# Inverse products spread over four row strips, and score products of a half gathered in one burst, in a two-layer hybrid trunk (pooling, retention, RWKV-7)

## The chip, the cores and the metric

The kernel runs on one core of a Trainium2 chip. The metric is the device time of one execution in microseconds. It is measured several times, and the median is taken. The profile is one further execution on the chip, taken by the hardware profiler.

The engines are named as in the profile: PE is TensorE (matmuls), PEld its weight loads, DVE VectorE, ACT ScalarE, POOL GpSimd, SP the queue that issues the DMAs. PSUM is the memory into which PE writes.

## What is computed

Two layers run one after the other on 1024 positions of 1024 channels, and a last RMSNorm follows. In a layer the normalised input goes through one wide projection, whose columns feed three token mixers: a causal pooling mixer, a retention mixer, and an RWKV-7 time mixer with 8 heads of 64 channels. Each mixer's output is gated, projected back, weighted by a sigmoid gate for each channel, summed, projected once more and added to the input. All is float32.

The change lies in the RWKV-7 mixer. Its definition goes step by step over the positions, with a 64 x 64 state S for each head:

```python
def step(S, inp):
    r_t, w_t, k_t, v_t, a_t, b_t = inp
    sa = jnp.einsum('bhvk,bhk->bhv', S, a_t)
    S = (S * w_t[:, :, None, :] + sa[..., None] * b_t[:, :, None, :]
         + v_t[..., None] * k_t[:, :, None, :])
    return S, jnp.einsum('bhvk,bhk->bhv', S, r_t)
_, y = lax.scan(step, jnp.zeros((B, H, N, N), jnp.float32), xs)
```

The kernel does it in chunks of 64 positions. In a chunk the recurrence is a triangular system, so each chunk and head needs the inverse of a 64 x 64 matrix that is the identity plus a strictly triangular part.

## The kernel before, in words

**The big projections.** The weights are streamed from DRAM in tiles (`wr`). Each tile is split into a high and a low part (`wh`, `wl`) of the fast fp32r type, and the activations are kept split in the same way (`hhi`, `hlo`). One fp32 product of 512 columns is then three fp32r matmuls into a PSUM tile `acc` (`mm3`). These acc products are most of PE's work and run all along.

**The RWKV task.** `rwkv_task` (line 1206 on) is called for a pair of heads, four times a layer, eight times in all. The heads of a pair lie in rows 0 to 63 and 64 to 127 of the tiles. A task has these stages, with 16 chunks of 64 positions:

- For each half of the sequence (8 chunks) it prepares the scaled operands `AR` and `BK`. LoRA products go into `lw` and `la`; transposes follow (`vt`, `bt`).
- *Score products g* (lines 1302 to 1318): BK times AR for each chunk and head, 64 rows deep and 128 x 128 in size. The two heads use the two 64-row halves of the array. Before, they come in two groups q of four chunks, eight products in each, into two PSUM tiles (one `mx`, one `cy`), and DVE masks them into `Z`, `GQ` and `KG` after each group.
- *The inverse* (lines 1338 to 1367): each 64 x 64 triangle is cut into four blocks of 32 x 32. DVE inverts the diagonal blocks by 30 elimination steps on `VB` and transposes the results into `GQ` and `N_` (a view of `Z`).
- *The products m1 and m2* (lines 1370 to 1390): the off-diagonal block of the inverse is (inverse of one diagonal block) x (off-diagonal block) x (inverse of the other), so two 32 x 32 products for each of 16 chunks x 2 heads. m1 reads rows 0 to 31, m2 reads rows 32 to 63. Each comes as two groups of 16, and ACT copies each group out of PSUM.
- *The chain over the chunks* (from line 1405): for c = 0 to 15 it alternates products `cy` and `ch` on PE with small copies on DVE and ACT. The first `ch` reads the finished inverse in `GQ`.

**What sets the order.** All operations are first recorded. The recording follows a clock of its own: the acc products call `pump()`, which lets tasks of the lanes ("rwkv", "mix", "norm", "post", "ada") record their next piece whenever its due time has come; `wait` delays a piece until the planner believes its inputs to be ready. `Prog.needs` then derives which operation depends on which. `Prog.weave` (line 406) is a list scheduler: it prices each operation (`Prog.cost`, line 347), and puts the operation of the engine that is free first next in the program. So each engine's order is fixed before the kernel runs, and on the chip each engine goes through it in that order. The helper at line 549 emits all instructions, so every row of the profile has this line, and the tiles' names tell the rows apart. The profile leaves out digits in names: m1 and m2 both read `m`, and `t_mq("mn")`, `t_mq("mt")` of the change read `mn` and `mt`.

The kernel divides PSUM into eight tiles of 512 columns: three `acc`, two `mx`, two `cy`, one `ch`.

Of the kernel before, what the change touches and what calls it, by code (L numbers as in the profile page):

```python
# [18 lines left out]
P = 128  # L19
# [187 lines left out]

class Op:
    __slots__ = ("eng", "what", "args", "kw", "outs", "ins", "prio", "lane", "pred", "succ", "n", "i",
                 "dur", "occ", "load", "twice", "lock", "est", "start", "end", "left", "table", "acc", "arr", "seq", "know", "waits", "part")  # L210


class Engine:
# [47 lines left out]
class Prog:  # L261


    def __init__(self):
        self.ops, self.bufs, self.width, self.pools = [], [], {}, {}
        self.now = lambda: 0.0
        self.lane = [None]
        for e in ENG:
            setattr(self, e, Engine(self, e))

# [40 lines left out]
    def needs(self):  # L311
        uses = {}
        for o in self.ops:
            for views, write in ((o.ins, False), (o.outs, True)):
                for v in views:
                    if v.tensor.key is not None:
                        uses.setdefault(v.tensor, []).append((o, v.mask(), write))
        for chain in self.chains.values():
            old = []
            for b in chain:  # L320
                w, r, mine = [], [], []
                for o, m, write in uses[b]:
                    free = True
                    for q, x in w:
                        if x & m and q is not o:
                            o.pred[q.i] = "d"
                            free = False
                    if not write:
                        r.append((o, m))
                    else:  # L330
                        for q, x in r:
                            if x & m and q is not o:
                                o.pred.setdefault(q.i, "a")
                                free = False
                        r = [(q, x & ~m) for q, x in r if x & ~m]
                        w = [(q, x & ~m) for q, x in w if x & ~m] + [(o, m)]
                    if free:
                        for q, wrote in old:
                            if q is not o:
                                o.pred.setdefault(q.i, "w" if wrote and write else "a")  # L340
                    mine.append((o, write))
                old = mine
        for o in self.ops:
            for q in o.pred:
                self.ops[q].succ.append(o.i)

    def cost(self, o):
# [6 lines left out]
        if o.eng == "PE":  # L354
            n = o.outs[0].free_size()
            rhs = o.ins[1]
            k = rhs.index.shape[0] * 32
            o.twice = rhs.dtype != F32R and w != "transpose"
            if rhs.dtype == F32R:
                o.load, o.occ, o.dur = (107, (n + 32) / 2.4, n / 2.4 + 176) if k == 128 else (55, 116, 393)  # L360
            elif k == 128:
                o.load, o.occ, o.dur = 109, 53, 273 if n > 1 else 250
            else:
                o.load, o.occ, o.dur = (55, 53, 272) if k == 64 else (32, 32, 191)
            return
        if o.eng == "SP":
            o.occ, o.dur = 470, 2100 if o.ins[0].space != DRAM and o.ins[0].tensor.key else 2650
# [38 lines left out]
    def weave(self):  # L406
# [9 lines left out]
        for o in ops:  # L416
            if not o.left:
                o.waits = []
                ready[o.eng].append(o)
        landed, table, pe = [0.0] * 8, 0, [0.0, 0.0]  # L420
        work = [0.0] * (int(WARM_UP / WINDOW) + 2)
        order = []
        other = {"DVE": "POOL", "POOL": "DVE"}
# [8 lines left out]
        while len(order) < len(ops):  # L432
# [23 lines left out]
            if e == "PE":  # L456
                k = int((s + 1000) / WINDOW) if s < WARM_UP else -1
                slow = 2 if k == 0 or k > 0 and work[k - 1] < 0.78 * WINDOW else 1
                ld, c = o.load * slow, c * slow
                m = max(pe[1], max(pe[0], o.est) + ld)  # L460
                if o.twice:
                    m += max(ld, c)
                if k >= 0:
                    work[k] += (m + c - max(s, pe[1])) * (1 if o.outs[0].free_size() > 1 else 0.1)
                pe[:] = m, m + c
                o.start, o.end = m, m + d + c - o.occ
            else:
                o.start, o.end = s, s + d
                free[e] = s + (d if e in over else c)
# [11 lines left out]
            for i in o.succ:  # L481
                p = ops[i]
                kind = p.pred[o.i]
                if p.eng != e or e == "SP":
                    r = o.end + SPACE_LAT[p.eng]
                elif kind != "a" and e != "PE":
                    r = o.end + SPACE_LAT[e]
                else:
                    r = s
                if r == s:  # L490
                    p.est = max(p.est, r)
                else:
                    a = p.arr.get(src, (0.0, 0, False))
                    p.arr[src] = max(a[0], r), max(a[1], o.seq), a[2] or kind == "d"
                    if kind == "d" and e != "SP":
                        for k, n in o.know.items():
                            if k != p.eng and n > p.know.get(k, 0):
                                p.know[k] = n
# [54 lines left out]
def trunk_kernel(ctx, tc, xT, cvec, pos, vecs, consts, w_ada, w_all, pool_w, lora_w, out):  # L553
# [19 lines left out]
    def nm(s):  # L573
        uid[0] += 1
        return f"{s}_{uid[0]}"
# [11 lines left out]
    t_mo = slot("mo", 4, HF + 16)  # L587
    t_vp = slot("vp", 2)
    t_cs = slot("cs", 3)
    mi = lambda s: t_mi(s)[:, 0:HF]  # L590
    mo = lambda s: t_mo(s)[:, 0:HF]

# [6 lines left out]

    def cyt(s):  # L600
        return ps_c.tile([P, HF], F32, tag="cy", name=nm(s))

    def hb(s):
        return hp_.tile([P, HF], F32R, tag="hb", name=nm(s))
# [601 lines left out]
    def rwkv_task(l, hp, kT, rT, vp, lt, lw):  # L1206
# [18 lines left out]
        for h in range(2):  # L1225
# [69 lines left out]
            for q in range(2):  # L1295
                ps = mx("bt")
                c0 = 8 * h + 4 * q
                for c in range(4):
                    trans(ps[:, c * P : (c + 1) * P], jt(BK, slice(0, P), c0 + c))
                nc.scalar.copy(BKt[:, c0 : c0 + 4, :], ps.rearrange("p (c n) -> p c n", n=P))  # L1300
                yield 1300
            for q in range(2):
                c0 = 8 * h + 4 * q
                yield wait(AR)
                gps = [mx("g"), cyt("g")]
                for j in range(4):
                    for hd in range(2):
                        rows = slice(64 * hd, 64 * hd + 64)
                        mmul(gps[hd][:, j * P : (j + 1) * P], jt(BK, rows, c0 + j), jt(AR, rows, c0 + j))
                lo, hi = slice(0, 64), slice(64, 128)  # L1310
                for hd in range(2):
                    own, other = (lo, hi) if hd == 0 else (hi, lo)
                    g3 = gps[hd].rearrange("p (u n) -> p u n", n=P)
                    c4 = slice(c0, c0 + 4)
                    nc.vector.tensor_tensor(Z[lo, c4, own], g3[lo, :, lo], rm(lo, lo), op=ALU.mult)
                    nc.vector.tensor_tensor(GQ[own, c4, hi], g3[lo, :, hi], rm(lo, hi), op=ALU.mult)
                    nc.vector.tensor_tensor(KG[other, c4, :], g3[hi, :, :], rm(hi, slice(0, P)), op=ALU.mult)
# [15 lines left out]
        def place_values(hd):  # L1333
            rows, cols = slice(64 - 64 * hd, 128 - 64 * hd), slice(64 * hd, 64 * hd + 64)
            nc.gpsimd.memset(VB[rows, :, 64 - 64 * hd : 128 - 64 * hd], 0.0)
            nc.scalar.copy(VB[rows, :, cols], Z[64:128, :, cols])

        place_values(0)
        for b in range(2):
            q = slice(32 * b, 32 * b + 32)  # L1340
# [20 lines left out]
            out=GQ[0:32, :, 0:64].rearrange("p a (b s) -> p s a b", s=32),  # L1361
            in_=M[0:32, :].rearrange("p (a b s) -> p s a b", s=32, b=2),
        )
        for b in range(2):
            q = slice(32 * b, 32 * b + 32)
            nc.vector.transpose(
                out=N_[q, :, q].rearrange("p u t -> p t u"), in_=M[q, :].rearrange("p (t s) -> p t s", s=32)
            )
        place_values(1)
        yield 2000  # L1370
        yield wait(Zt, G)
        for q in range(2):
            ps = mx("m1")
            for u in range(16):
                uu = 16 * q + u
                mmul(ps[32:64, u * 32 : u * 32 + 32], N_[0:32, uu, 32:64], t1(slice(0, 32), uu))
                if u % 16 == 15:
                    yield 600
            nc.scalar.copy(GQ[32:64, 8 * q : 8 * q + 8, 0:64], ps[32:64, :].rearrange("p (c n) -> p c n", n=64))
        yield wait(G)  # L1380
        for q in range(2):
            ps = mx("m2")
            for u in range(16):
                uu = 16 * q + u
                mmul(ps[0:32, u * 32 : u * 32 + 32], t1(slice(32, 64), uu), N_[32:64, uu, 32:64])
                if u % 16 == 15:
                    yield 600
            nc.scalar.copy(
                N_[0:32, 16 * q : 16 * q + 16, 32:64], ps[0:32, :].rearrange("p (u s) -> p u s", s=32)
            )  # L1390
        nc.vector.tensor_copy(GQ[0:64, :, 0:64], Z[0:64, :, 0:64])
        nc.scalar.copy(GQ[64:128, :, 0:64], Z[0:64, :, 64:128])
        SS = [sp.tile([P, P], F32, tag="S", name=nm("S"), bufs=2) for _ in range(2)]
        for S in SS:
            nc.gpsimd.memset(S, 0.0)
# [9 lines left out]
        for c in range(16):  # L1405
# [13 lines left out]
            if c < 15:  # L1419
                cy_next = own_values(c + 1)  # L1420
            yield wait(xst)
            ch = ps_c.tile([P, HF], F32, tag="ch", name=nm("ch"), bufs=1)
            mmul(ch[:, 0:P], GQ[:, c, :], xst)
            nc.vector.tensor_copy(Z[0:64, c, :], ch[0:64, 0:P])
            for hd in range(2):
# [712 lines left out]
```

## Time and profile before

| | |
|---|---|
| median of 3 runs | 2336.88 us (2336.01 to 2342.26) |
| the profiled execution's own time | 2333.52 us |
| its span, first to last instruction | 2331.7 us |
| granted TensorE clock, mean | 0.996 of full speed |
| DRAM traffic over the span | 97 GB/s |

In the profile the busy time of an engine is a share of the span. A weight load (PEld) overlaps the matmuls (PE). A matmul row's length is that of one instruction through the pipeline, and the next one starts long before it ends, so the cost of a matmul is read from start to start. An fp32 matmul appears as two records, one for each pass, and an fp32r matmul as one. A row of the timeline with a count holds that many records one after the other.

### The profile page before, as it was taken

What the parts mean: (1) busy time and instruction counts of PE and PEld (TensorE: products, weight loads), DVE (VectorE), ACT (ScalarE), POOL (GpSimd) and SP (SyncE); (2) the same over time, 40 slices, a digit from 0 to 9 for tenths busy, and PEclk for the clock granted to TensorE, in tenths of its full rate; (3) what the DMA queues carried; (4) which work ended last, traced back from release to release, by engine and by line L of the source; (5) the groups of instructions that cost most, each with busy time, mean ns of one, the idle gap of its engine ahead of it and who ended that gap; (6) DMA issues with size and microseconds to landing.
All of it is one profiled execution on the core that took longest, in us unless ns stands there. A gap on an engine that the chain in (4) does not pass through costs nothing. (4 is left out here: it accounts for less than half of the span.)

```text
span 2331.7 us, 33818 instructions
## 1 busy us (share of the span) xinstructions
PE 2287.5 (98%) x12520; PEld 1907.6 (82%) x12520; DVE 1442.1 (62%) x2826; ACT 855.8 (37%) x1706; POOL 817.4 (35%) x714
## 2 busy tenths in 40 slices
PE   5999999999999999999999999999999999999998
PEld 4888888888888888888887888888788888888888
DVE  8776578468568744669546746855864884413544
ACT  5633442433433333223444334234433423311343
POOL 5222233234142333463442233323323333326441
PEclk9999999999999999999999999999999999999999
DMA  8132112112213325767422211211211131545442
GB/s 283 39 110 78 42 46 92 42 41 70 73 55 99 102 61 178 237 194 250 139 82 64 69 41 44 94 34 49 78 61 42 56 118 52 162 126 163 118 145 82
DMA packets 126517, 227.79 MB, mean 98 GB/s; under 512 B 14352, under 2 KB 17680, under 8 KB 126352
## 3 DMA queue, kind: packets, MB, share of 16 engines
q1 hardware_dynamic: 126352, 225.63, 30.9%
q8 instruction: 98, 1.61, 0.3%
q14 instruction: 67, 0.55, 0.1%
HBM read 176.56 MB, written 49.02 MB: 97 GB/s over the span
## 5 line engine op out<-in xcount | busy, mean ns | idle before, releaser
L549 PE MATMUL acc<-hhi,wh 128*128 128x512 f32 x2000 | 806.7, 403 | 0.0
L549 PE MATMUL acc<-hhi,wl 128*128 128x512 f32 x2000 | 806.6, 403 | 0.0
L549 POOL TENSOR_TENSOR wl<-wr,wh 128x512 fp32r<-128x512 f32 x342 | 458.5, 1341 | 991.4 <-ACT wh L549 947.3
L549 PE MATMUL acc<-hlo,wh 128*128 128x512 f32 x2000 | 805.1, 403 | 0.0
L549 ACT CAST wh<-wr 128x512 fp32r<-128x512 f32 x342 | 212.2, 620 | 655.2 <-PE acc L549 441.7
L549 PEld LDWEIGHTS acc<-hlo,wh 128*128 128x128 f32 x2000 | 378.0, 189 | 66.6 <-issue 2.2
L549 PEld LDWEIGHTS acc<-hhi,wl 128*128 128x128 f32 x2000 | 378.1, 189 | 66.5 <-issue 2.2
L549 PEld LDWEIGHTS acc<-hhi,wh 128*128 128x128 f32 x2000 | 378.2, 189 | 65.6 <-issue 1.1
L549 PE MATMUL acc<-oG,wl 128*128 128x512 f32 x384 | 149.9, 390 | 0.0
L549 PE MATMUL acc<-oG,wh 128*128 128x512 f32 x384 | 149.7, 390 | 0.0
L549 PE MATMUL acc<-olo,wh 128*128 128x512 f32 x384 | 149.7, 390 | 0.0
L549 DVE SCALAR_TENSOR_TENSOR S<-ch,pc,SP 64x64 f32<-64x64 f32 x224 | 63.3, 282 | 91.3 <-PE ch L549 85.2
L549 ACT COPY xst<-Z 64x64 f32<-64x64 f32 x256 | 62.4, 244 | 152.7 <-DVE Z L549 149.5
L549 DVE COPY xst<-cy 64x64 f32<-64x64 f32 x256 | 55.4, 216 | 90.7 <-PE cy L549 65.2
L549 DVE TENSOR_TENSOR tm<-VB 64x30 f32<-64x30 f32 (+14 forms) x240 | 105.4, 439 | 7.4
L549 DVE TENSOR_TENSOR VB<-VB,tm 64x30 f32<-64x30 f32 (+14 forms) x240 | 99.4, 414 | 7.5
L549 DVE COPY Z<-ch 64x128 f32<-64x128 f32 x128 | 36.0, 282 | 93.1 <-PE ch L549 92.5
L549 ACT ACTIVATE gsg<-acc 128x512 f32<-128x512 f32 x88 | 52.4, 596 | 91.9 <-PE acc L549 79.6
L549 PEld LDWEIGHTS acc<-olo,wh 128*128 128x128 f32 x384 | 72.1, 188 | 15.0
L549 PEld LDWEIGHTS acc<-oG,wh 128*128 128x128 f32 x384 | 72.1, 188 | 15.0 <-DVE gs L549 0.2
L549 PEld LDWEIGHTS acc<-oG,wl 128*128 128x128 f32 x384 | 72.1, 188 | 15.0
L549 DVE SCALAR_TENSOR_TENSOR gs<-gs,acc 128x512 f32<-128x512 f32 x64 | 43.7, 684 | 46.1 <-PE acc L549 45.0
(270 smaller groups left out, 3693.6 us busy)
## 6 DMA issues: line engine op xcount, KB each, us to landing
wr<-in_w_all SPq DMA_DIRECT2D x364, 256.0 KB, 2.7
gd<-gsg SPq DMA_DIRECT2D x88, 256.0 KB, 2.0
gs<-gd SPq DMA_DIRECT2D x88, 256.0 KB, 2.8
wada<-in_w_ada SPq DMA_DIRECT2D x70, 256.0 KB, 3.3
ol<-od SPq DMA_DIRECT2D x64, 256.0 KB, 3.2
ringG<-in_w_ada SPq DMA_DIRECT2D x26, 256.0 KB, 5.1
x<-in_xT SPq DMA_DIRECT2D x16, 256.0 KB, 5.0
od<-po SPq DMA_DIRECT2D x16, 256.0 KB, 2.2
```

The source lines that it names most:

```text
L549: f(*[put(x) for x in o.args], **{k: put(x) for k, x in o.kw.items()})
```

## The change

The score products of one half of the sequence are issued together: sixteen products into four PSUM tiles (`mx`, `cy`, `ch`, `cy`) where before there were two groups of eight, each with two tiles. DVE masks them after that, in the same operations as before.

The products m1 and m2 are spread over the four strips of 32 rows. Strip g holds one head of the pair and one half of the chunks (the list `quad`): eight products in each strip. The operands of three of the four strips are therefore copied into two new tiles `mn` and `mt` (W1 and W2 in the code) by ACT and DVE, partly before the inversion, partly after it. The products of a step are issued as one list of 32, in which each product is on another strip than the one before. Each strip has its own PSUM tile. Each result is copied out in four pieces of 32 x 256, two by ACT and two by DVE, where before there were two pieces by ACT. The result of m2 now goes straight into `GQ`, and the copies of the diagonal blocks into `GQ` are recorded between the two steps.

For the scheduler, the products of such a list are recorded as a burst: each product of a burst is given the dependences of all of them, so that the list starts when all its operands are there. The price of a pass with 32 rows goes from 32 to 15 ns, and a change of the number of rows between two products costs 110 ns (to 32 rows) or 200 ns.

```diff
+        for a, b in self.bursts:
+            own = [o for o in self.ops[a:b] if o.eng == "PE"]
+            union = {q for o in own for q in o.pred if not a <= q < b}
+            for o in own:
+                for q in union:
+                    o.pred.setdefault(q, "x")
...
-                o.load, o.occ, o.dur = (55, 53, 272) if k == 64 else (32, 32, 191)
+                o.load, o.occ, o.dur = (55, 53, 272) if k == 64 else (15, 15, 191)
...
+                if o.rows != rows:
+                    m, rows = m + (110 if o.rows == 32 else 200), o.rows
...
-                elif kind != "a" and e != "PE":
+                elif kind in "dw" and e != "PE":
...
+            yield wait(AR)
+            gps = [[mx("g"), cyt("g")], [cht("g"), cyt("g")]]
+            at = len(nc.ops)
             for q in range(2):
-                c0 = 8 * h + 4 * q
-                yield wait(AR)
-                gps = [mx("g"), cyt("g")]
                 for j in range(4):
                     for hd in range(2):
-                        rows = slice(64 * hd, 64 * hd + 64)
-                        mmul(gps[hd][:, j * P : (j + 1) * P], jt(BK, rows, c0 + j), jt(AR, rows, c0 + j))
-                lo, hi = slice(0, 64), slice(64, 128)
+                        rows, c = slice(64 * hd, 64 * hd + 64), 8 * h + 4 * q + j
+                        mmul(gps[q][hd][:, j * P : (j + 1) * P], jt(BK, rows, c), jt(AR, rows, c))
+            nc.bursts.append((at, len(nc.ops)))
...
+        W1, W2 = t_mq("mn"), t_mq("mt")
+        quad = [(slice(32 * g, 32 * g + 32), g // 2, slice(8 * (g % 2), 8 * (g % 2) + 8)) for g in range(4)]
+        q4 = lambda t, rows, j=0: t[rows, 256 * j : 256 * j + 256].rearrange("p (c s) -> p c s", s=32)
+        for rows, hd, c8 in quad[1:]:
+            nc.scalar.copy(q4(W1, rows), Z[0:32, c8, 64 * hd + 32 : 64 * hd + 64])
...
+        for i, (rows, hd, c8) in enumerate(quad[1:]):
+            (nc.scalar.copy, nc.vector.tensor_copy)[i % 2](
+                q4(W1, rows, 1), GQ[0:32, c8, 32 * hd : 32 * hd + 32]
+            )
...
+        for i, (rows, hd, c8) in enumerate(quad):
+            if i != 1:
+                nc.scalar.copy(q4(W2, rows, 1), Z[32:64, c8, 64 * hd + 32 : 64 * hd + 64])
...
-        for q in range(2):
-            ps = mx("m1")
-            for u in range(16):
-                uu = 16 * q + u
-                mmul(ps[32:64, u * 32 : u * 32 + 32], N_[0:32, uu, 32:64], t1(slice(0, 32), uu))
-                if u % 16 == 15:
-                    yield 600
-            nc.scalar.copy(GQ[32:64, 8 * q : 8 * q + 8, 0:64], ps[32:64, :].rearrange("p (c n) -> p c n", n=64))
...
+        def quads(name, lhsT, rhs):
+            pss = [mx(name), cyt(name), cht(name), cyt(name)]
+            at = len(nc.ops)
+            for v in range(8):
+                for g, (rows, hd, c8) in enumerate(quad):
+                    u, o = 2 * (c8.start + v) + hd, slice(32 * v, 32 * v + 32)
+                    mmul(pss[g][rows, o], lhsT(g, rows, u, o), rhs(g, rows, u, o))
+            nc.bursts.append((at, len(nc.ops)))
+            return pss
...
+        for g, (rows, hd, c8) in enumerate(quad):
+            (nc.scalar.copy, nc.vector.tensor_copy)[g % 2](W2[rows, 0:256], pss[g][rows, 0:256])
+        nc.scalar.copy(GQ[64:128, :, 0:64], Z[0:64, :, 64:128])
+        nc.vector.tensor_copy(GQ[0:64, :, 0:64], Z[0:64, :, 0:64])
...
+        for g, (rows, hd, c8) in enumerate(quad):
+            (nc.scalar.copy, nc.vector.tensor_copy)[g % 2](
+                GQ[64 * hd : 64 * hd + 32, c8, 32:64], q4(pss[g], rows)
+            )
```

The order of instructions on PE in the first task, where m1 stands. Before (m_325 and m_326 are m1's two PSUM tiles, m_327 the first of m2; the acc rows are the projections that run beside it):

```order
L549 MATMUL acc_1761<-hhi_551,wl_1723 128x512
L549 MATMUL m_325_1814<-G_1077,Z_918 32x32 x16
L549 MATMUL acc_1761<-hhi_606,wh_1717 128x512
L549 MATMUL acc_1761<-hlo_618,wh_1717 128x512
L549 MATMUL acc_1761<-hhi_606,wl_1723 128x512
L549 MATMUL m_326_1838<-G_1077,Z_918 32x32 x16
L549 MATMUL acc_1761<-hhi_627,wh_1717 128x512
```

After, at the same place (m_327 to m_330 are the four strips' tiles of m1; mn_1166 is W1; eight such rounds follow each other):

```order
L561 MATMUL acc_1793<-hlo_532,wh_1677 128x512
L561 MATMUL m_327_1812<-G_1082,Z_919 32x32
L561 MATMUL m_328_1815<-mn_1166 32x32
L561 MATMUL m_329_1817<-mn_1166 32x32
L561 MATMUL m_330_1819<-mn_1166 32x32
L561 MATMUL m_327_1812<-G_1082,Z_919 32x32
```

The two groups of sixteen, which had three acc products between them, have become one list of 32 in which the strip changes at every row. Nine acc products now stand between the end of m1 and the start of m2.

The order on ACT around the copies of m1's and m2's results in the same task, before (G_1077 holds GQ, Z_918 holds Z; the copy into VB places values for the chain):

```order
L549 COPY G_1077<-m_325_1814 32x8x64
L549 COPY VB_1496<-Z_918 64x16x64
L549 COPY G_1077<-m_326_1838 32x8x64
L549 ACTIVATE gsg_1862<-acc_1761 128x512
L549 COPY Z_918<-m_327_1864 32x16x32
L549 COPY Z_918<-m_328_1886 32x16x32
L549 COPY G_1077<-Z_918 64x16x64
```

and after (mt_1808 is W2; m_331 and m_333 are two of m2's four tiles):

```order
L561 COPY mt_1808<-Z_919 32x256
L561 COPY mt_1808<-m_327_1812 32x256
L561 COPY VB_1466<-Z_919 64x16x64
L561 COPY mt_1808<-m_329_1817 32x256
L561 COPY G_1082<-Z_919 64x16x64
L561 COPY G_1082<-m_331_1871 32x8x32
L561 COPY G_1082<-m_333_1875 32x8x32
```

The copies out of PSUM have become smaller and go to W2 first. The copy of 64x16x64 into GQ has moved ahead of the copies of m2's result, and the copy into VB stands between the two of m1 as before.

More of the change, by code (lines that the diff above doesn't have):

```diff
@@ L209 @@
     __slots__ = ("eng", "what", "args", "kw", "outs", "ins", "prio", "lane", "pred", "succ", "n", "i",
-                 "dur", "occ", "load", "twice", "lock", "est", "start", "end", "left", "table", "acc", "arr", "seq", "know", "waits", "part")
+                 "dur", "occ", "load", "twice", "lock", "est", "start", "end", "left", "table", "acc", "arr", "seq", "know", "waits", "part", "rows")
 class Engine:
@@ L267, in __init__ @@
         self.lane = [None]
+        self.bursts = []
         for e in ENG:
@@ L358, in cost @@
             o.twice = rhs.dtype != F32R and w != "transpose"
+            o.rows = k
             if rhs.dtype == F32R:
@@ L419, in weave @@
                 ready[o.eng].append(o)
-        landed, table, pe = [0.0] * 8, 0, [0.0, 0.0]
+        landed, table, pe, rows = [0.0] * 8, 0, [0.0, 0.0], 128
         work = [0.0] * (int(WARM_UP / WINDOW) + 2)
@@ L489, in weave @@
                     r = s
-                if r == s:
+                if kind == "x":
+                    p.est = max(p.est, r)
+                elif r == s:
                     p.est = max(p.est, r)
@@ L589, in trunk_kernel @@
     t_cs = slot("cs", 3)
+    t_mq = slot("mq", 2)
     mi = lambda s: t_mi(s)[:, 0:HF]
@@ L601, in cyt, with cht @@
         return ps_c.tile([P, HF], F32, tag="cy", name=nm(s))
+    def cht(s):
+        return ps_c.tile([P, HF], F32, tag="ch", name=nm(s), bufs=1)
     def hb(s):
@@ L1301, in rwkv_task @@
                 yield 1300
+            yield wait(AR)
+            gps = [[mx("g"), cyt("g")], [cht("g"), cyt("g")]]
+            at = len(nc.ops)
             for q in range(2):
-                c0 = 8 * h + 4 * q
-                yield wait(AR)
-                gps = [mx("g"), cyt("g")]
                 for j in range(4):
                     for hd in range(2):
-                        rows = slice(64 * hd, 64 * hd + 64)
-                        mmul(gps[hd][:, j * P : (j + 1) * P], jt(BK, rows, c0 + j), jt(AR, rows, c0 + j))
-                lo, hi = slice(0, 64), slice(64, 128)
+                        rows, c = slice(64 * hd, 64 * hd + 64), 8 * h + 4 * q + j
+                        mmul(gps[q][hd][:, j * P : (j + 1) * P], jt(BK, rows, c), jt(AR, rows, c))
+            nc.bursts.append((at, len(nc.ops)))
+            lo, hi = slice(0, 64), slice(64, 128)
+            for q in range(2):
+                c4 = slice(8 * h + 4 * q, 8 * h + 4 * q + 4)
                 for hd in range(2):
                     own, other = (lo, hi) if hd == 0 else (hi, lo)
-                    g3 = gps[hd].rearrange("p (u n) -> p u n", n=P)
-                    c4 = slice(c0, c0 + 4)
+                    g3 = gps[q][hd].rearrange("p (u n) -> p u n", n=P)
                     nc.vector.tensor_tensor(Z[lo, c4, own], g3[lo, :, lo], rm(lo, lo), op=ALU.mult)
@@ L1363, in rwkv_task @@
         )
-        for b in range(2):
+        for i, (rows, hd, c8) in enumerate(quad[1:]):
+            (nc.scalar.copy, nc.vector.tensor_copy)[i % 2](
+                q4(W1, rows, 1), GQ[0:32, c8, 32 * hd : 32 * hd + 32]
+            )
+        for b in (1, 0):
             q = slice(32 * b, 32 * b + 32)
@@ L1368, in rwkv_task @@
             )
+        for i, (rows, hd, c8) in enumerate(quad):
+            if i != 1:
+                nc.scalar.copy(q4(W2, rows, 1), Z[32:64, c8, 64 * hd + 32 : 64 * hd + 64])
         place_values(1)
-        yield 2000
-        yield wait(Zt, G)
-        for q in range(2):
-            ps = mx("m1")
-            for u in range(16):
-                uu = 16 * q + u
-                mmul(ps[32:64, u * 32 : u * 32 + 32], N_[0:32, uu, 32:64], t1(slice(0, 32), uu))
-                if u % 16 == 15:
-                    yield 600
-            nc.scalar.copy(GQ[32:64, 8 * q : 8 * q + 8, 0:64], ps[32:64, :].rearrange("p (c n) -> p c n", n=64))
@@ L1380, in rwkv_task @@
[L1380 to L1389, printed above, removed]
-            )
-        nc.vector.tensor_copy(GQ[0:64, :, 0:64], Z[0:64, :, 0:64])
@@ L1392, in rwkv_task @@
-        nc.scalar.copy(GQ[64:128, :, 0:64], Z[0:64, :, 64:128])
+        def quads(name, lhsT, rhs):
[7 more added lines that the diff above has]
+            return pss
@@ new lines, in rwkv_task @@
+        half2 = lambda t, rows, o: t[rows, 256 + o.start : 256 + o.stop]
+        yield 1000
+        yield wait(W1, G)
+        pss = quads(
+            "m1",
+            lambda g, rows, u, o: W1[rows, o] if g else N_[0:32, u, 32:64],
+            lambda g, rows, u, o: half2(W1, rows, o) if g else t1(rows, u),
+        )
+        for g, (rows, hd, c8) in enumerate(quad):
+            (nc.scalar.copy, nc.vector.tensor_copy)[g % 2](W2[rows, 0:256], pss[g][rows, 0:256])
+        nc.scalar.copy(GQ[64:128, :, 0:64], Z[0:64, :, 64:128])
@@ new lines, in rwkv_task @@
+        nc.vector.tensor_copy(GQ[0:64, :, 0:64], Z[0:64, :, 0:64])
+        yield 800
+        yield wait(W2)
+        pss = quads(
+            "m2",
+            lambda g, rows, u, o: W2[rows, o],
+            lambda g, rows, u, o: half2(W2, rows, o) if g != 1 else N_[32:64, u, 32:64],
+        )
+        for g, (rows, hd, c8) in enumerate(quad):
+            (nc.scalar.copy, nc.vector.tensor_copy)[g % 2](
+                GQ[64 * hd : 64 * hd + 32, c8, 32:64], q4(pss[g], rows)
+            )
@@ L1421, in rwkv_task @@
             yield wait(xst)
-            ch = ps_c.tile([P, HF], F32, tag="ch", name=nm("ch"), bufs=1)
+            ch = cht("ch")
             mmul(ch[:, 0:P], GQ[:, c, :], xst)
```

## Prediction

> **What bounds the kernel now.** I read the page first, then what TensorE (PE) waits for, then the timeline around the products that the change touches.
>
> ```profile
> span 2331.7 us, 33818 instructions
> PE 2287.5 (98%) x12520; PEld 1907.6 (82%) x12520; DVE 1442.1 (62%) x2826; ACT 855.8 (37%) x1706; POOL 817.4 (35%) x714
> ```
>
> Its waits, longest in total first (us in total, times, longest):
>
> ```profile
> PE acc L549 <- DVE sq L549: 20.1, 3, 12.0
> PE rot L549 <- DVE yc L549: 5.1, 2, 2.8
> PE adaps L549 <- DVE ada_acc L549: 4.5, 3, 2.2
> PE acc L549 <- ACT hhi L549: 2.1, 1, 2.1
> PE cy L549 <- ACT y L549: 1.2, 4, 0.3
> ```
>
> PE is busy 98% of the span. The largest wait, 20.1 us, is the start-up; after it no wait for another engine is over 5.1 us in total, and none for the tiles g, m1 or m2 is listed. PE is in order and always has projection work (acc) behind it, so a microsecond taken out of its queue should come off the end.
>
> The next rows are the first group of inverse products (the trace drops digits, so m1 and m2 both read m). Columns: start, length, engine, then the instruction and its count.
>
> ```profile
> 204.68 0.39 PE L549 MATMUL acc<-hhi,wl 128*128 128x512 f32 x1
> ...
> 207.40 0.39 PE L549 MATMUL acc<-hhi,wl 128*128 128x512 f32 x1
> 207.72 1.19 PE L549 MATMUL m<-G,Z 32*32 32x32 f32 x32
> 208.84 0.50 PE L549 MATMUL acc<-hhi,wh 128*128 128x512 f32 x1
> 209.18 0.40 PE L549 MATMUL acc<-hlo,wh 128*128 128x512 f32 x1
> ...
> 405.47 0.39 PE L549 MATMUL acc<-hhi,wh 128*128 128x512 f32 x1
> 405.79 2.21 PE L549 MATMUL m<-G,Z 32*32 32x32 f32 x64
> 407.93 0.50 PE L549 MATMUL acc<-hlo,wh 128*128 128x512 f32 x1
> 408.26 0.40 PE L549 MATMUL acc<-hhi,wl 128*128 128x512 f32 x1
> ```
>
> From 204.68 to 207.40 lie twelve equal steps, so an acc product costs 0.227 us. An fp32 product runs as two passes (the 256 products g have 512 records, below), so the row x32 is sixteen products. From 207.40 to 209.18 are 1.78 us; less two acc steps (0.454), the excursion cost 1.326. Where both m1 groups stood together (x64, 405.47 to 408.26) it cost 2.79 − 0.454 = 2.336. The difference, 1.010 us for 32 passes, gives **31.6 ns a pass**, and 1.326 − 1.010 = **0.316 us for going into the 32-row form and back**.
>
> The score products g, eight in a group, on two strips of 64 rows in turn:
>
> ```profile
> 118.59 0.40 PE L549 MATMUL acc<-hhi,wl 128*128 128x512 f32 x1
> 118.92 1.16 PE L549 MATMUL g<-AR,BK 64*128 64x128 f32 x16
> 120.01 0.50 PE L549 MATMUL acc<-hhi,wh 128*128 128x512 f32 x1
> 120.35 0.40 PE L549 MATMUL acc<-hlo,wh 128*128 128x512 f32 x1
> ```
>
> The weight loads of the same group, and those of all groups (shortest, median and longest in ns):
>
> ```profile
> 118.92 0.97 PEld L549 LDWEIGHTS g<-AR,BK 64*128 64x128 f32 x16 [0.36 <-issue]
> ...
> L549 PEld LDWEIGHTS g<-AR,BK x512: 182/188/188, 118.9 to 1874.9; 64*128 64x128 f32 x171
> ```
>
> The excursion cost 120.35 − 118.59 − 0.454 = 1.306 us. Sixteen loads of 0.188 fit into 0.97, so the two strips run side by side: eight rounds of two passes, seven of them in 0.97 − 0.188 = 0.782, 0.112 a round. Eight rounds are 0.894, which leaves **0.41 us for into the 64-row form and back**.
>
> **The change, part by part.** Counted in the two programs' orders, before has 256 m1, 256 m2 and 256 g products, and after has the same. What moves is their grouping. The order rows in the section on the change show it for the first task: in m1, sixteen products on one strip, three acc products, and sixteen more have become 32 in one piece that change strip at every product. Counting each change of form through both orders, excursions into the 32-row form go from 25 to 16, into the 64-row form from 51 to 36 (g from 34 to 16, the lw and la products from 17 to 20).
>
> *Fewer excursions.* 9 × 0.316 = 2.8 us and 15 × 0.41 = 6.2 us, together 9.0. No idle time covered these, so this is a gain by itself; only the waits below could take it back.
>
> *Passes on four strips.* The trace has no four-strip products, so I bound them. No overlap leaves 31.6 ns: gain 0. Four strips fully side by side, as the two strips of g are, give 31.6 / 4 = 7.9 ns: 1024 passes × 23.7 = 24.3 us. A pairwise overlap, the only one that a row shows, gives 15.8 ns: 1024 × 15.8 = **16.2 us**. I take the last. In the new program both passes of a product stand on one strip before the next strip's product comes, so if passes start in program order, the second pass holds the next strip back by one load, and only two strips are ever at work. The planner's new price for such a pass is 15 ns; its old one was 32 where the trace has 31.6, and its other new constants (110 and 200 ns, 0.31 together) meet my 0.316, so its prices tend to be near the chip. That makes the same value likelier without showing it.
>
> The Trainium skill, "TensorE: Matmul & The Clock Gate", section "Part 3: Packing small matmuls — row/col tiling", says that matmuls start and end in strict program order and only weight loads are pulled ahead; by that rule the sum is the 15.8 one, and no row here tells it from 7.9.
>
> *Copies added.* Comparing the orders of ScalarE (ACT) and VectorE (DVE) by group, ACT gets 96 copies of 32x256 and loses 32 of 32x512, DVE gets 40 of 32x256. The nearest rows:
>
> ```profile
> L549 ACT COPY G<-m 32x512 f32<-32x512 f32 x16 | 9.2, 578 | 20.5 <-PE m L549 20.4
> L549 ACT COPY VB<-Z 64x1024 f32<-64x1024 f32 x16 | 16.7, 1045 | 18.6 <-PE g L549 16.6 <-DVE Z L549 1.8
> L549 DVE TENSOR_TENSOR Z<-g,cst 64x256 f32<-64x256 f32 x64 | 26.6, 416 | 48.9 <-PE g L549 47.5
> ```
>
> At 0.58 and 0.42 at most that is up to 56 − 18 = 38 us more for ACT and 17 for DVE, on engines at 37% and 62%. It costs nothing while PE has acc products to run. Where PE could stand is at m2, which waits for all four copies of m1's result. Nine acc products stand between (2.04 us). On ACT the order there (shown with the change) is copy, the 1.05 us value copy VB, copy: at 0.58 each 2.21 us, at half that (half the elements) 1.63. On DVE it is two copies, 0.84. So m2 is covered or late by about 0.2 us; eight times that is 1.4 us, the bound. The next is the first ch product, which needs m2's result: two ACT copies, at most 1.16 us, under seven acc and two cy products, over 2.0 us. I enter 0 for both. The g burst needs four PSUM tiles at once, so its masking on DVE is released later by one round, while 32 acc products follow it; 0 too. Three weight-gate tiles fewer are sent early through DRAM (82 writes for 88): transfers, not PE work, and PE waits for none.
>
> The sum: 9.0 + 16.2 = 25.2 us off the profiled run, 2333.5 us (span 2331.7 and 1.8 around it): 2308.3. The median of the runs, 2336.88, is 3.4 above the profiled one; from it 2336.9 − 25.2 = **2311.7 us**.
>
> **Rivals.**
>
> *Four strips really at once (7.9 ns).* For it: in g both strips finish a load in every round, so strips as such do not disturb each other. Against it: the order of the passes, above. Gain 9.0 + 24.3 = 33.3, time 2303.6. Chance 0.17.
>
> *Strips bring nothing for passes this short.* If the gap between passes is set by their issue and not by the strip's own load, 31.6 ns stays, only the excursions are saved: 9.0, time 2327.9. For it: 31.6 ns is the shortest steady spacing in the trace. Against it, the two-strip products lw and la start 0.01 us apart:
>
> ```profile
> 135.38 0.49 PE L549 MATMUL lw<-lt,lw 64*128 64x512 f32 x1
> 135.39 0.49 PE L549 MATMUL la<-lt,lw 64*128 64x512 f32 x1
> 135.72 0.39 PE L549 MATMUL lw<-lt,lw 64*128 64x512 f32 x1
> 135.72 0.39 PE L549 MATMUL la<-lt,lw 64*128 64x512 f32 x1
> ```
>
> That is pairs of starts, not a steady stream. Chance 0.18, for it and the values between it and 15.8. The Trainium skill, same page, section "Wait — 56ns, not 53.3ns?", has a floor of about 25 ns from start to start however small the product; by that rule the sum would be an estimated 1024 × 6.6 = 6.8 plus 9.0, time 2321.1. The pair of rows above, at 10 ns, speaks against that floor across strips.
>
> *Slower: PE stands at the head of its bursts.* Every burst now waits for all its operands before its first product, and the chain m1, copies, m2, copies, first ch has more copies in it. If ACT or DVE come late, PE stands with all acc work queued behind. There are 24 such places (m1, m2, first ch, in eight tasks); from 25.2 / 24 = 1.05 us a place on, the change loses. If each stood for as long as the nine acc products again, 2.04 us, that is 49.0 − 25.2 = 23.8 slower, 2360.7. For it: the 0.2 us that I found at m2. Against it: PE never waited for m before, and the margins above. Chance 0.06.
>
> *No change that shows.* Half of these waits, with little from the strips: about 2335. Chance 0.04. That the bursts would be torn apart again by the planner is excluded by the order.
>
> **How the numbers follow.** The forecast has chance 0.55, 2311.7 with some 3 us either way for the 1.4 us at m2 and waits such as the 5.1 us at rot, which fall differently in a new order. The predicted time is its: 2312. A range from 2302 (four strips at once, a little more) to 2326 leaves out the far half of the second rival (0.09), the slower one and the last one (0.10). The measurement can tell about 0.3%, 7 us, so faster is under 2329.9: 0.55 + 0.17 and 0.14 of the second rival, less 0.01, 0.85. The rest of the second rival and the fourth case are the same: 0.09. Slower: 0.06.
>
> **What would show it.** In the profile after, an m row of x64 lasting 1.0 us + 0.2 rather than 2.21 says 15.8 ns; about 0.7 says 7.9; about 2.2 says no overlap. The g rows should come as x32 and cost 1.306 + 0.894 = 2.20 us between acc products, less two acc steps. PE's busy time should fall by about 25 us, its waits stay near what they are. The forecast is wrong if new rows for m, ch or g above 5 us appear in the list of PE's waits, or if PE's own sum falls by less than 15.

## The result and the profile after

The changed kernel took **2300.38 us** (median of 4 runs, 2299.89 to 2304.04) beside 2336.45 us for the kernel before: ratio 0.9846, 95% interval 0.9825 to 0.9867. It is faster by 36 us, where 25 were forecast, and the time lies 1.6 us below the forecast range. The profiled execution took 2304.04 us.

```profile
span 2302.3 us, 33923 instructions
PE 2254.6 (98%) x12520; PEld 1881.8 (82%) x12520; DVE 1454.2 (63%) x2866; ACT 874.3 (38%) x1770; POOL 817.9 (36%) x714
```

PE still has 98% of the span: the span fell by 29.4 us and PE's busy time by 32.9. ACT has 18.5 us more work and DVE 12.1. PE's longest waits after the change:

```profile
PE acc L561 <- DVE sq L561: 20.2, 3, 12.0
PE rot L561 <- DVE yc L561: 6.3, 2, 4.5
PE adaps L561 <- DVE ada_acc L561: 4.1, 2, 2.2
...
PE m L561 <- DVE mn L561: 0.6, 1, 0.6
...
PE m L561 <- DVE mt L561: 0.2, 1, 0.2
```

All rows of this list together are 40.7 us, against 36.9 before. The new ones for m are 0.8 us, and no row for ch or g is in it.

The first list of 32 inverse products (G,Z is the first strip's operand, mn that of the other three):

```profile
207.85 0.39 PE L561 MATMUL acc<-hlo,wh 128*128 128x512 f32 x1
208.17 0.21 PE L561 MATMUL m<-G,Z 32*32 32x32 f32 x1
208.18 0.23 PE L561 MATMUL m<-mn 32*32 32x32 f32 x3
208.22 0.19 PE L561 MATMUL m<-G,Z 32*32 32x32 f32 x1
208.23 0.20 PE L561 MATMUL m<-mn 32*32 32x32 f32 x3
208.26 0.19 PE L561 MATMUL m<-G,Z 32*32 32x32 f32 x1
208.26 0.20 PE L561 MATMUL m<-mn 32*32 32x32 f32 x3
208.29 0.19 PE L561 MATMUL m<-G,Z 32*32 32x32 f32 x1
...
208.85 0.50 PE L561 MATMUL acc<-hhi,wl 128*128 128x512 f32 x1
209.19 0.39 PE L561 MATMUL acc<-hhi,wh 128*128 128x512 f32 x1
```

In each of these rounds of 0.032 us, the time of one pass before, all four strips start a pass; in the second half of the list the starts come 8.3 to 8.4 ns apart. The excursion costs 209.19 − 207.85 − 0.454 = 0.886 us; less 0.316 for the change of form, 0.570 for 64 passes: **8.9 ns a pass**. That is the list without a wait in it: seven of the sixteen lists cost 0.88 to 0.90 us, the other nine 0.99 to 1.69. Before, two groups of sixteen cost 2 × 1.326.

The first list of score products:

```profile
121.47 0.40 PE L561 MATMUL acc<-hhi,wl 128*128 128x512 f32 x1
121.80 2.06 PE L561 MATMUL g<-AR,BK 64*128 64x128 f32 x32
123.78 0.50 PE L561 MATMUL acc<-hhi,wh 128*128 128x512 f32 x1
124.12 0.39 PE L561 MATMUL acc<-hlo,wh 128*128 128x512 f32 x1
```

124.12 − 121.47 − 0.454 = 2.196 us, where 2.20 was forecast.

### The profile page after: what moved, and what is told of

Same layout as the page of the kernel before. It is cut to its first block, busy times and chain, and to the rows that moved or that the text cites. A ratio compares the mean times of both kernels' runs of the same rounds, so it can differ in the third digit from the quotient of the medians.

```text
span 2302.3 us, 33923 instructions
## 1 busy us (share of the span) xinstructions
PE 2254.6 (98%) x12520; PEld 1881.8 (82%) x12520; DVE 1454.2 (63%) x2866; ACT 874.3 (38%) x1770; POOL 817.9 (36%) x714
## 4 chain that ended last, share of the span: by engine, by line
PE 88%; DVE 7%; issue 2%; DMA 1%; ACT 1%; POOL 0%; SPq 0%; DVEq 0%; ACTq 0%; POOLq 0%
PE acc L561 73%; PE cy L561 4%; PE ch L561 2%; PE g L561 1%; PE ro L561 1%; DVE VB L561 1%; DVE ada_ps L561 1%; DVE tm L561 1%; DVE ada_acc L561 1%; DVE Z L561 1%; PE rs L561 1%; PE rkv L561 1%; PE bt L561 1%; DVE G L561 1%; PE lw L561 1%
## 5 line engine op out<-in xcount | busy, mean ns | idle before, releaser
L561 DVE SCALAR_TENSOR_TENSOR mrg<-gs,acc 128x512 f32<-128x512 f32 x32 | 21.9, 686 | 99.4 <-PE acc L561 99.4
```

The lines of the kernel that those rows point to most:

```text
L561: f(*[put(x) for x in o.args], **{k: put(x) for k, x in o.kw.items()})
```

## The experiments

### One part alone

In the first kernel the score products stay as before:

```diff
...
-            gps = [[mx("g"), cyt("g")], [cht("g"), cyt("g")]]
...
             for q in range(2):
+                c0 = 8 * h + 4 * q
+                yield wait(AR)
+                gps = [mx("g"), cyt("g")]
...
```

Expected: 

> The changed kernel with the score products as before (two groups of eight a half); only m1 and m2 lie on four strips. Theory A (the gain is PE time of the products themselves: passes on four strips overlap and excursions are fewer): an m excursion costs about 1.0 us as in the profile of the changed kernel, 16 of them 16 us instead of 40, and the program's order has 54 excursions into the 64-row form for 51, so 24.3 - 1.2 = 23 us faster than before, about 2313. Rival B (a good part of the gain comes from the other order of the rest, the planner's prices, and not from the products): about 30 us faster, 2306 or less, since the planner's prices are all in.

Measured: 2308.65 us, ratio 0.9889 (0.9869 to 0.9909) to 2334.16: 25.5 us faster.

In the second, m1 and m2 are as before, and the price is again 32:

```diff
...
-        pss = quads(
-            "m1",
...
+        for q in range(2):
+            ps = mx("m1")
+            for u in range(16):
+                uu = 16 * q + u
+                mmul(ps[32:64, u * 32 : u * 32 + 32], N_[0:32, uu, 32:64], t1(slice(0, 32), uu))
...
```

Expected: 

> The changed kernel with m1 and m2 as before (one strip, groups of 16, the old price of 32 ns); only the score products of a half come as one list of sixteen. Theory A: 34 excursions into the 64-row form for 51, 17 x 0.41 = 7.0 us less, two more into the 32-row form, 0.6 us more: 6.4 us faster than before, about 2330. Rival B (the order of the rest): 10 to 12 us faster, about 2325.

Measured: 2325.87 us, ratio 0.9963 (0.9946 to 0.998): 8.3 us faster.

The two parts add up: 25.5 + 8.3 = 33.8. Theory A's numbers, 23 and 6.4, lie inside both intervals. But so do rival B's, 30 at the edge of the first and 10 to 12 in the second, so these times alone do not decide. The profiles of the kernel before and of the changed one do. Each excursion is priced as above, from the acc start ahead of it to the second start behind it, less two acc steps. Over all excursions, m cost 43.0 us before and 16.8 after, g 44.2 and 34.7, lw and la 18.1 and 19.2. That is 34.6 us less, so most of the gain is the products' own time. Of the 43.0, 2.5 us come from a halved clock, told below. The 25.5 are the part that the prediction put at 19.0 (16.2 for the passes, 2.8 for the excursions).

### The order inside a list

The same products on the same strips, with the same copies, in another order. Strip by strip:

```diff
-            for v in range(8):
-                for g, (rows, hd, c8) in enumerate(quad):
+            for g, (rows, hd, c8) in enumerate(quad):
+                for v in range(8):
...
```

Expected: 

> The changed kernel, but a list of 32 inverse products goes strip by strip: eight products on the first strip, then eight on the second, and so on; the data, the copies and the planner's prices stay. Theory A1 (passes of different strips overlap only where they stand close together in the program): 64 passes at 31.6 ns and 0.3 us for the excursion, 2.34 us a list instead of 1.0, 16 x 1.34 = 21 us slower than the changed kernel. Rival A2 (each strip draws its own passes from far ahead, so the order inside a list does not matter): 1.0 us a list, no difference. Between them, a look-ahead of about two strips' worth gives 1.3 us a list, 5 us slower.

Measured: 2311.73 us, ratio 0.9902 (0.9884 to 0.9921). A list of this kernel:

```profile
206.83 0.39 PE L561 MATMUL acc<-hlo,wh 128*128 128x512 f32 x1
207.15 0.59 PE L561 MATMUL m<-G,Z 32*32 32x32 f32 x13
207.55 0.21 PE L561 MATMUL m<-mn 32*32 32x32 f32 x1
207.58 0.19 PE L561 MATMUL m<-G,Z 32*32 32x32 f32 x1
207.61 0.19 PE L561 MATMUL m<-mn 32*32 32x32 f32 x1
207.61 0.19 PE L561 MATMUL m<-G,Z 32*32 32x32 f32 x1
207.64 0.19 PE L561 MATMUL m<-mn 32*32 32x32 f32 x1
207.64 0.19 PE L561 MATMUL m<-G,Z 32*32 32x32 f32 x1
207.67 1.39 PE L561 MATMUL m<-mn 32*32 32x32 f32 x45
208.98 0.50 PE L561 MATMUL acc<-hhi,wl 128*128 128x512 f32 x1
209.32 0.40 PE L561 MATMUL acc<-hhi,wh 128*128 128x512 f32 x1
```

The list costs 209.32 − 206.83 − 0.454 = 2.036 us, so 26.9 ns a pass: nearly one strip's rate. A2 falls, and A1 holds with a small look-ahead that these rows show. All sixteen passes on the first strip (G,Z) stand ahead of the second strip's in the program. Yet the second strip's first pass starts at 207.55, when only thirteen of them have started; the three left follow one by one, each beside a pass of the second strip. In these rows PE thus starts passes of another strip some three passes early, and overlaps them no further than that. In time, the kernel lost 10 to 11 us on the changed kernel, not 16 × 1.0 to 1.15. The profiles show the price of the lists all the same: PE's busy time is 15.6 us above the changed kernel's (2267.3 us, and 2251.7 in the profile of its next measurement, told below), the span 12.8 us; PE idles 2.8 us less in the other order, and two excursions into the 64-row form are saved.

Two strips at a time:

```diff
-            for v in range(8):
-                for g, (rows, hd, c8) in enumerate(quad):
+            for v, (g, (rows, hd, c8)) in [
+                (v, (g, quad[g])) for two in ((0, 1), (2, 3)) for v in range(8) for g in two
+            ]:
+                if True:
...
```

Expected: 

> The changed kernel, but a list of 32 inverse products first alternates between the strips 0 and 1 (sixteen products), then between 2 and 3. Theory A1 (the strips that stand next to each other in the program work side by side, each at 31.6 ns a pass): 15.8 ns a pass, 1.33 us a list instead of 1.0, 16 x 0.33 = 5 us slower than the changed kernel. Theory of the prediction (never more than two strips at work whatever the order): no difference from the changed kernel.

Measured: 2301.69 us, ratio 0.9861 (0.9843 to 0.988). A list of this kernel:

```profile
391.66 0.39 PE L561 MATMUL acc<-hhi,wl 128*128 128x512 f32 x1
391.98 0.21 PE L561 MATMUL m<-G,Z 32*32 32x32 f32 x1
391.98 0.21 PE L561 MATMUL m<-mn 32*32 32x32 f32 x1
392.03 0.19 PE L561 MATMUL m<-G,Z 32*32 32x32 f32 x1
...
392.47 0.61 PE L561 MATMUL m<-mn 32*32 32x32 f32 x29
393.01 0.50 PE L561 MATMUL acc<-hhi,wh 128*128 128x512 f32 x1
393.35 0.40 PE L561 MATMUL acc<-hlo,wh 128*128 128x512 f32 x1
```

1.69 − 0.454 = 1.236 us, 14.4 ns a pass. This is what the prediction's 15.8 looks like, and it needs two strips in the program; four give 8.9. The time itself does not show theory A1's 5 us: it agrees with the prediction's theory, no difference. The lists do not agree with it: all sixteen cost 23.1 us here and 16.8 in the changed kernel. What the order outside the lists gave back was not followed up.

### A longer list

```diff
-            for v in range(8):
+            for v in [*range(8), *range(8)]:
...
```

Each list of 32 is issued twice, with the same results written again.

Expected: 

> The changed kernel with each list of 32 inverse products issued twice in one piece (the second time writes the same results again), to price passes on four strips in a longer list. Theory S (four strips at work all the time): the second half costs 64 x 7.9 to 8.9 ns, 0.51 to 0.57 us, on top of the 1.0 us of a list. Theory Q (the first half of a list starts from instructions that already lie in PE's queue, and later ones come at the rate at which they are issued): first passes at 7.9 ns, later ones at 9.3 ns or more, so 0.6 us or more on top, and the spacing grows along the list. Rival of the prediction (15.8 ns): 1.0 us on top.

Measured: 2316.24 us in one run, and a list without a wait in it:

```profile
592.97 0.40 PE L561 MATMUL acc<-hhi,wl 128*128 128x512 f32 x1
593.29 0.21 PE L561 MATMUL m<-mt 32*32 32x32 f32 x1
...
594.51 0.50 PE L561 MATMUL acc<-hhi,wh 128*128 128x512 f32 x1
594.85 0.39 PE L561 MATMUL acc<-hlo,wh 128*128 128x512 f32 x1
```

1.88 − 0.454 = 1.426, so the second 64 passes cost 1.426 − 0.886 = 0.540 us, 8.4 ns each. Theory S holds: four strips work all the time. The starts come 7.9 ns apart in the second sixteen passes, 9.6 in the third and 8.3 to 8.4 from there to the end, so theory Q's growing spacing is not seen. The time is 15 us above the changed kernel's 2301.22, where 16 × 0.54 is 8.6: six of the sixteen lists cost over 2.0 us, with PE idle for 0.2 to 0.5 us in each of them.

### The granted clock

What the sum with 8.9 ns leaves over was looked for in the clock. In the profile of before, the granted clock stood at one half for 10 us right behind the second group of m1 in the sixth task:

```profile
1524.64 1.19 PE L549 MATMUL m<-G,Z 32*32 32x32 f32 x32
1525.76 0.64 PE L549 MATMUL acc<-hhi,wl 128*128 128x512 f32 x1
1526.20 0.63 PE L549 MATMUL acc<-hhi,wh 128*128 128x512 f32 x1
1526.62 0.63 PE L549 MATMUL acc<-hlo,wh 128*128 128x512 f32 x1
```

and over ten us each ahead of, during and after that place (the number ahead of the last two is the clock):

```profile
1516.00:1526.00 10.00, 10.00 (x98) 8.11 (x97) 8.77 (x12) 3.80 (x7) 2.42 (x3) 1.00 0.17 54
1526.00:1536.00 10.00, 10.00 (x78) 7.64 (x78) 0.69 (x1) 3.25 (x5) 1.26 (x1) 0.50 0.10 26
1536.00:1546.00 10.00, 10.00 (x54) 8.43 (x53) 3.88 (x12) 3.86 (x11) 1.47 (x2) 0.99 0.09 19
```

The acc products there start 0.43 us apart instead of 0.227, with PE busy all the time. To provoke it, the kernel before issues each m1 and m2 product twice on its one strip:

```diff
-                mmul(ps[32:64, u * 32 : u * 32 + 32], N_[0:32, uu, 32:64], t1(slice(0, 32), uu))
+                for _ in range(2):
+                    mmul(ps[32:64, u * 32 : u * 32 + 32], N_[0:32, uu, 32:64], t1(slice(0, 32), uu))
...
```

Expected: 

> The kernel before with each of the inverse products m1 and m2 issued twice on its one strip (the same result written again): 1024 more passes. Theory A (products only): 1024 x 31.6 ns = 32.4 us slower than before, 2367 to 2369. Theory C (long stretches of 32-row products lower the granted clock): also more time at half clock, right after or in such lists, visible as a second pitch of 0.43 us between acc products there; each such stretch of 3.4 to 10 us costs half its length, so 40 us or more slower.

Measured: 2414.19 us, ratio 1.033 (1.0305 to 1.0354): 78.6 us slower, where the passes alone are 32.4. The stretch around the first task's lists:

```profile
205.00:212.00 7.00, 7.00 (x109) 5.74 (x108) 2.85 (x2) 2.24 (x3) 2.17 (x2) 1.00 0.20 57
212.00:229.00 17.00, 17.00 (x187) 14.27 (x184) 0.69 (x1) 4.35 (x7) 0.28 (x1) 0.51 0.05 17
229.00:240.00 11.00, 11.00 (x63) 9.45 (x62) 3.29 (x13) 3.56 (x12) 2.28 (x2) 0.99 0.22 65
```

Its mean clock fell to 0.972 (0.996 before). In seven of the eight tasks the clock stood at one half for 17.07 us, from the lists of m1 on; the profile of before has one such place, of 10.24 us. A list of 64 passes costs 3.8 us there, beside two acc steps at 0.43 us, and 2.34 us at full clock. In the seventh task the same four lists ran at full clock throughout. Theory C holds for longer stretches of 32-row products on one strip: in most of them the clock halves, and stays so for some microseconds behind. What decides whether it does is not shown.

How much of this the kernel before has seems to differ from run to run: one of its executions was profiled, and of the others only the mean clock is known. In the ten profiles taken of kernels whose lists run over the strips (those told further down included), no halving directly follows a list. What is left stands at the start, at the end and behind a longer wait of PE, such as the one for rot; the nearest to a list begins 5.6 us behind it, with a wait of 2.33 us for pdh between, in the kernel with the longer list. The kernel with the old m1 and m2 and the new score products has again 10 us at half clock, behind its m1 in the fifth task, and 3.4 us right behind m in the eighth.

The changed kernel, measured twice more:

Expected: 

> The changed kernel itself once more, timed beside the kernel before on one chip, to size what is left over. Theory A (products only): 9.0 us for the excursions and 1024 passes x (31.6 - 8.9) = 23.2 us, 32 us in all, ratio 0.9862. Theory C (on top of that the long lists on one strip make the granted clock fall to one half for some microseconds after them in many executions, and the short lists do not): 34 to 38 us, ratio 0.984 to 0.9855.

Measured: 2301.22 us, ratio 0.9854 (0.9839 to 0.987), 34.4 us from 2335.64. The ratio lies in theory C's range, but theory A's 0.9862 lies inside the interval too.

Expected: 

> The changed kernel a third time, as the measure for the two kernels beside it. Theory A with C (products 32 us, and some 2 to 4 us less time at half clock): ratio to before 0.984 to 0.987, and at equal granted clock 31 to 32 us from before.

Measured: 2301.76 us, ratio 0.9857 (0.9836 to 0.9878), 30.6 us from 2332.32.

The runs can be sorted by their mean clock. In the first of these two sets, the kernel before took 2334.35, 2335.75 and 2335.64 us at 0.996, and the changed one 2303.04 at 0.996: 32.2 apart. The kernel before took 2330.05 at 0.998 and 2338.58 at 0.993. In the second set the four runs of before at 0.996 have a mean of 2332.9, the two of the changed kernel 2302.3: 30.6 apart. In that set the fastest at 0.998, 2330.16 and 2300.06, are 30.1 apart, and the single ones at 0.995, 2336.41 and 2301.22, 35.2. So at equal clock the change is worth some 30 to 32 us, one pair aside, near theory A's 32, and up to a few more where the kernel before is caught at half clock. The mean clock is a rough measure, since it also holds the halvings at the start, at the end and behind PE's long waits. Whether 36, 34 or 31 is seen depends on that and on the spread; the intervals overlap from 0.984 to 0.987. A kernel before without the halvings was not tried, so this last share is read from the runs' clocks and not from an edit.

### The planner's price

```diff
-                o.load, o.occ, o.dur = (55, 53, 272) if k == 64 else (15, 15, 191)
+                o.load, o.occ, o.dur = (55, 53, 272) if k == 64 else (8, 8, 191)
```

Expected: 

> The changed kernel with the planner's price of a 32-row pass at 8 ns instead of 15, near what the profile shows. The products are the same, only the order around the lists is planned for a shorter list. Theory A (the gain is PE's own time): no difference from the changed kernel, ratio to before 0.984 to 0.987. Rival B (the planner's order makes a good part of it): 3 us or more away from the changed kernel.

Measured: 2296.4 us, ratio 0.9834 (0.9818 to 0.9849); all its four runs lie below all four of the changed kernel in the same set, at the same clock. Once more:

Expected: 

> The changed kernel with the planner's price of a 32-row pass at 8 ns, once more, to tell whether the 4.8 us from the changed kernel repeat. Theory P (the order planned with the price near the chip's leaves fewer waits inside and in front of the lists, and the rest of the order falls well): 4 to 5 us faster than the changed kernel in all rounds. Rival N (run-to-run spread): within 2 us of it.

Measured: 2296.25 us, ratio 0.9839 (0.9817 to 0.9861), 5.5 us below the changed kernel, with one run in four at 2301.3. So rival B has a part: the order around the lists, planned with a price near the chip's, is worth some 5 us, and theory A's "no difference" falls. In the profiles of the first set, 3.7 us apart, the lists account for 1.3 us of it (16.7 and 15.4 in all: most of the changed kernel's lists have a short wait in them, with a median of 0.99 us against the 0.886 above, most of this kernel's have none), and PE's waits for 0.9 (38.7 against 39.6). The rest is spread over small rows and not located.

A last kernel also records the LoRA products as a burst:

```diff
+        at = len(nc.ops)
         for i, (a, b) in enumerate(((0, 0), (0, 1), (1, 0))):
             for j in range(2):
                 own = slice(64 * j, 64 * j + 64)
                 mmul(pss[j], lw[a][own, hc], lt[b][own, :], start=(i == 0), stop=(i == 2))
+        nc.bursts.append((at, len(nc.ops)))
```

Expected: 

> The kernel with the price of 8 ns, and the six LoRA products lw and la of a half also recorded as one burst, so that the planner does not split them: 34 excursions into the 64-row form instead of 36. Theory A (an excursion costs 0.41 us): 0.8 us faster than the price of 8 ns alone, which is hard to see. Rival B (the new order moves more than that): over 2 us either way.

Measured: 2295.85 us, ratio 0.983 (0.981 to 0.9851). 0.4 us from the price alone, which the spread hides. Theory A's 0.8 can't be told from nothing, and rival B's 2 us is not seen.

## Why the prediction was wrong

- **The bound** was right: PE had all the work before and after, and what left its queue came off the end.
- **Fewer excursions, 9.0 us:** right. The traces have the counts that were forecast, 25 and 16 excursions into the 32-row form, 51 and 36 into the 64-row form. The g lists cost the forecast 2.20 us. With the score products alone 8.3 us (interval 4.7 to 12.6) were measured where 6.4 were expected of that kernel.
- **Passes on four strips, 16.2 us: this step failed.** It said that "if passes start in program order, the second pass holds the next strip back by one load, and only two strips are ever at work". They do not start in that order: up to three older passes of another strip are overtaken in the strip-by-strip rows. If the two passes of a product stand next to each other, which no view shows, that is just as far as the fourth strip's first pass must be pulled ahead. Four strips ran at 8.9 ns a pass, 1024 × (31.6 − 8.9) = 23.2 us, 7.0 more than the term. The rule of the Trainium skill that was brought in for it ("TensorE: Matmul & The Clock Gate", "Part 3: Packing small matmuls — row/col tiling": matmuls in strict program order) does not agree with the strip-by-strip rows, where passes of the second strip start ahead of three older ones of the first. The prediction held that no row told 15.8 from 7.9, but the trace of before already spoke for the rival: the sixteen loads of the first g group start in eight pairs, 6 to 7 ns inside a pair and 0.108 to 0.112 us from pair to pair, and its sixteen passes start in eight pairs too. So both strips were at work from the first pair to the last. With passes held to the order that the prediction assumed, the first pass of a group and the last would have stood alone.
- **The planner's price of 15** was counted as a hint; the chip's is 8.4 to 8.9. That its other constants fit the trace said nothing about this one.
- **The mended sum** is 9.0 + 23.2 = 32.2 us, 2304.7 from the median that was used, 4.3 us above the measured time. The rival with four strips at once had the mechanism, at 7.9 ns and 2303.6. The range's lower end, 2302, allowed for it but for little else.
- **The clock was missed.** The halving behind the m1 groups of the sixth task stood in the trace of before, as acc products 0.43 us apart. The two groups of m2 inside that stretch cost 2.1 us each, beside two acc steps at 0.43 us, for 1.33 at full clock. It would explain why the runs of before spread over 2330 to 2342 us and why the median gain came out up to 4 us above the mended sum; this is read from the mean clocks and not shown by an edit.
- **Copies at no cost:** nearly right. The ACT copies took 0.36 us, not the bound of 0.58, and PE idled 0.8 us in all for m. But the sixteen lists cost 16.8 us, 2.6 more than 16 × 0.886. The first m2 list shows one such wait: it started at 211.13, and the copy for its third strip ended at 211.22. With these 2.6 the mended sum is 29.6 us, near the 30 to 32 at equal clock. The slower rival never had a place: no wait for m, ch or g came near 5 us.
- **No overlap for short passes:** refuted, at 8.4 ns from start to start in a list of 64 products, and with it the estimate of 2321.1 us.

## What to carry to other kernels

Where small products share an array, put neighbours in the program on different strips: the same 32 products cost 0.89 us in rotation over four strips, 1.24 over two and 2.04 strip by strip. In the kernel's time four strips and two could not be told apart here. Count the excursions into another row form as work of their own (0.3 to 0.4 us each). And before summing, look along the trace of a PE-bound kernel for stretches in which the big products run at twice their spacing, since what sets them off may be the very instructions that a change removes.

## What had not been expected of the hardware

- Passes on different strips pass each other in time: a strip's first pass started beside the thirteenth of another strip's sixteen, which all stood ahead of it. So PE does not keep the program's order across strips. How the two passes of an fp32 product are laid down in the final program is not shown by any view, so how far PE looks ahead is known only from this one case, about three passes.
- A PE that the profile shows busy can still lose its clock. PE was busy 100% of the time in the windows above, and the granted clock still went to 0.5: 17 us at a time, in seven of eight tasks, where each task issued four groups of 32 small products (64 passes each) on one strip. In the ten profiles with lists spread over the strips, no halving directly followed a list. What the granted clock goes by is not shown.
